# Scaling softmax weights with diagonal matrices on TensorE, and pairing complex products on VectorE, in a one-core decoder layer

## The chip, the cores and the metric

The kernel runs on one core of one Trainium2 chip. The metric is the device time of one execution in microseconds (us); the median of three runs is compared. One further execution was recorded by the hardware profiler, and all rows below are from it. The engines are named as in the profile: PE is TensorE (PEld its weight loads), DVE VectorE, ACT ScalarE, POOL GpSimd, SP SyncE.

## The reference, cut to what matters

The layer has 512 tokens of width 1024 and one depth. An attention with three branches (compressed, selected, window) and a state-space model run side by side on the normalised input; their outputs are mixed, and a channel mixer (PEER) picks 128 experts per token out of 16384. With 512 tokens every selection block is kept, so the selected and the window branch are both causal attention over all earlier tokens. The lines that the change touches compute this:

```
e = where(mask, exp(s - max(s)), 0);  p = e / max(sum(e), 1e-30)      # softmax of a branch
o = gate * (p @ v)                                                  # 8 heads, 2 kv heads
lam_bar = exp(lam * dt)                                             # complex, 32 groups x 64 states
b_bar = ((lam_bar - 1) / lam) * bmat
state[t] = lam_bar * state[t-1] + b_bar @ u[t];  y[t] = Re(cmat @ state[t])
h = h + concat(attention, ssm) @ w_out
h = h + sum over 8 heads x 16 experts of gelu(x . u_e) * gate_e * v_e  # PEER
```

## The kernel before, in words

Tokens are cut into four blocks of 128 (T = 0 to 3). The Python code emits instructions in an order of its own, and a list scheduler, which works with a timing model of the chip, then puts the instructions of each engine into a fixed order. Only the dense stage at the end is kept in program order (`ordered`). Scratch memory comes from slots: `M.L` is a slot of 2048 columns, `M.S` a quarter of one, and who takes a slot waits for whoever used it last.

The stages, in order of time:

- **Parameters and the first block (about 0 to 220 us).** `Half` (two objects, 16 state-space groups each) builds from the parameters the tables PB (b_bar times powers of lam_bar; steps i = 2, 1, 0), CL (the same for c, on POOL) and MT (powers of the unit part of lam_bar, doubled in seven steps k = 0 to 6, each 8 x 2^k columns wide). PB and MT are made on DVE by `cmul`, six VectorE operations for one complex product. Meanwhile PE projects the input. `compress` makes the compressed keys of block 0; it begins with four additions of a position table (`c_peT`) on DVE, in whose output 32 matrix products on PE are waiting. Then come the state-space output, block 0's attention, its mix and its routing.
- **The rest, woven with PEER (about 220 to 735 us).** `rest` projects the other blocks, runs attention(1), the mix of block 1, then the routing of block 1 woven with attention(2) and attention(3), and at last the routing of blocks 2 and 3. Between these, steps of `peer` are emitted by a credit that each piece of work earns. One step gathers a row of `uv` for each of 128 tokens (1 MB, an indirect DMA issued by POOL), takes a dot product on DVE (the operation that writes `junk` and `hid`), five short ACT operations (`gt`, `act`) and a multiply-add on DVE, or from the 109th step on a product on PE (`dg`). Five slots hold gathered rows; a gather is issued two steps ahead, and the multiply-add runs two steps behind.
- **The dense stage (about 850 us to the end).** Blocks 2 and 3 go through all experts by matrix products; 113 steps of block 1 are spread through it.

Inside `attention(T)`, for each of the four pairs (kv head g, branch br), `scores` makes for four heads the scores on PE, their maximum on DVE (`nm`), the exponential with its sum on ACT (`Pt`, `sm`), and three small DVE operations that turn the sums into factors sm. It then multiplies each head's weights (128 rows x N = 128(T+1) columns) by its column of factors: on DVE for T = 0, 1, 2, on ACT for T = 3 (`PSC`). `pv` transposes each 128 x 128 piece of `Pt` on PE against the identity matrix (`c_ident`), copies four of them out of PSUM and multiplies by the values.

Of the kernel before, what the change touches and what calls it, by code (L numbers as in the profile page):

```python
# [18 lines left out]
AF = mybir.ActivationFunctionType  # L19
ALU = mybir.AluOpType  # L20
# [143 lines left out]
def hymba_kernel(ctx: ExitStack, tc: tile.TileContext, a, out, dbg=None):  # L164
# [94 lines left out]
    def cmul(e, outr, outi, xr, xi, yr, yi, t1, t2):  # L259
        e.tensor_tensor(t1, xr, yr, op=ALU.mult)  # L260
        e.tensor_tensor(t2, xi, yi, op=ALU.mult)
        e.tensor_tensor(outr, t1, t2, op=ALU.subtract)
        e.tensor_tensor(t1, xr, yi, op=ALU.mult)
        e.tensor_tensor(t2, xi, yr, op=ALU.mult)
        e.tensor_tensor(outi, t1, t2, op=ALU.add)


    lam = const("lam", [128, 3, 16])
    gmask = const("gmask", [128, 2], eng=G)
# [10 lines left out]
    ident = const("ident", [128, 128])  # L280
# [134 lines left out]
    class Half:  # L415


        def __init__(self, hf, small):
# [11 lines left out]
            cmul(V, pb4[0], pb4[1], br, bi, wr, wi, s1.v(sh4), s2.v(sh4))  # L430
            lbr = lb[:, 0, hs, None].to_broadcast([128, 8, 32])
            lbi = lb[:, 1, hs, None].to_broadcast([128, 8, 32])
            for i in (2, 1, 0):
                cmul(V, PB[0][:, :, i], PB[1][:, :, i], PB[0][:, :, i + 1], PB[1][:, :, i + 1], lbr, lbi,
                     s1.v([128, 8, 32]), s2.v([128, 8, 32]))

            CL = [c.v([128, 8, 5, 32]) for c in self.cl]
            gm = gmask[:, None, :, None].to_broadcast(sh4)
# [12 lines left out]
            MT = [self.mt.v([128, 8, 128], off=4096 * i) for i in range(2)]  # L451
            V.memset(MT[0][:, :, 0:1], 1.0)
            V.memset(MT[1][:, :, 0:1], 0.0)
            for k in range(7):
                n = 1 << k
                sh = [128, 8, n]
                cmul(V, MT[0][:, :, n:2 * n], MT[1][:, :, n:2 * n], MT[0][:, :, 0:n], MT[1][:, :, 0:n],
                     am[:, k, 0, hs, None].to_broadcast(sh), am[:, k, 1, hs, None].to_broadcast(sh), s1.v(sh), s2.v(sh))
# [226 lines left out]
    kcF, vcF = ct("kcF", [128, 2, 31]), ct("vcF", [31, 2, 64])  # L685


    PSC = lambda T, h: T > 2
    PCP = lambda T, kb: T < 3 and kb % 2
    AT, ST, XN, EI, GA = {}, {}, {}, {}, {}  # L690

    def attention(T):
# [13 lines left out]
        sh = [128, 8, n31]  # L706
# [14 lines left out]
        def scores(g, br):  # L721
            pl = M.S() if T == 0 else M.L((0, 1))
            Pt = pl.v([128, 4, N])
            nm = tiny.tile([128, 4], F32, name="nm")
            sm = tiny.tile([128, 4], F32, name="sm")
            for h in range(4):
                par, i = h % 2, h // 2
                ps = bank()
                rows = slice(64 * par, 64 * par + 64)
                PE.matmul(ps[:, 0:N], qT[T][rows, 2 * g + i], KT[rows, 2 * br + g, 0:N], start=True, stop=False)  # L730
                PE.matmul(ps[:, N - 128:N], identb, maskb, start=False, stop=True)
                V.reduce_max(nm[:, h:h + 1], ps[:, 0:N], axis=AX.X, negate=True)
                S.activation(Pt[:, h], ps[:, 0:N], AF.Exp, bias=nm[:, h:h + 1], accum_out=sm[:, h:h + 1])
                bfree(ps)
            V.tensor_scalar(sm, sm, 1e-30, None, op0=ALU.max)
            V.reciprocal(sm, sm)
            V.tensor_tensor(sm, sm, gts[:, T, 4 * g:4 * g + 4, 1 + br], op=ALU.mult)
            for h in range(4):
                if PSC(T, h):
                    S.activation(Pt[:, h], Pt[:, h], AF.Copy, scale=sm[:, h:h + 1])  # L740
                else:
                    V.tensor_scalar(Pt[:, h], Pt[:, h], sm[:, h:h + 1], None, op0=ALU.mult)
            return pl, Pt

        def pv(g, br, pl, Pt):
            for kb in range(T + 1):
                b = bank()
                pt = b3(b, 128)
                for h in range(4):
                    PE.transpose(pt[:, 2 * (h % 2) + h // 2], Pt[:, h, kb * 128:kb * 128 + 128], ident)  # L750
                ps = M.S()
                PT = ps.v([128, 4, 128])
                if PCP(T, kb):
# [6 lines left out]
                              PT[:, 2 * par:2 * par + 2], start=(br == 0 and kb == 0), stop=False, skip_group_check=True)  # L760
                M.free(ps)
                yield
            M.free(pl)

        prev = None
        for g in range(2):
# [884 lines left out]
```

## Time and profile before

| what | value |
|---|---|
| median of 3 runs | 1618.69 us (1617.03 to 1622.68) |
| the profiled execution's own time | 1620.03 us |
| its span, first to last instruction | 1618.2 us |
| PE, DVE, ACT, POOL busy | 1367.1, 1475.7, 837.0, 521.8 us |
| instructions | 24071 |

The busy times are sums over stages with different limits, so they say little by themselves; what counts is which engine is full in a stage and what the chain of waits runs through there. A PE that is called busy need not run at its peak: PEclk is the clock granted to it as a share of full speed, 1.0 for 2.4 GHz and 0.5 for 1.2 GHz.

### The profile page before, as it was taken

To read this page: it belongs to the slowest core of one execution; us is meant where nothing else is said; L and a number is where in the kernel's file an instruction comes from. 1 tells how busy PE (TensorE), PEld (TensorE's weight loads), DVE (VectorE), ACT (ScalarE), POOL (GpSimd) and SP (SyncE) were. 2 spreads that over 40 slices of the span, in tenths; PEclk is the share of its full clock that TensorE was granted. 3 is DMA by queue.
4 is the path that set the end of the run, shared out by engine and by line. 5 is a ranking of instruction groups with operands and counts; after the bars stand their busy time and mean duration, and the time that the engine had idled before them with its cause. 6 is when DMAs were issued, how large, how long until landed. Compare 5 with 4: busy or idle time off the path is not lost.

```text
span 1618.2 us, 24071 instructions
## 1 busy us (share of the span) xinstructions
PE 1367.1 (84%) x8256; PEld 1081.8 (67%) x8256; DVE 1475.7 (91%) x3392; ACT 837.0 (52%) x2046; POOL 521.8 (32%) x383
## 2 busy tenths in 40 slices
PE   5687794588946689696579999999999999999996
PEld 2366572454433455682358888888888999999995
DVE  8986279969899999699999999999999999999998
ACT  2335523545455675225565555555555556555553
POOL 6422013745354233003002333333333433333331
PEclk9897898787877789899859999999999999999998
DMA  6331478888998989309707999999999999999994
GB/s 263 104 105 65 169 278 295 330 321 300 375 352 297 345 356 370 152 6 343 248 4 262 338 345 332 342 337 340 333 346 357 392 375 377 374 375 379 375 376 171
DMA packets 88967, 469.45 MB, mean 290 GB/s; under 512 B 10253, under 2 KB 10893, under 8 KB 50701
## 3 DMA queue, kind: packets, MB, share of 16 engines
q0 software_dynamic: 37152, 268.98, 42.7%
q1 hardware_dynamic: 51692, 198.94, 34.3%
q8 instruction: 64, 1.05, 0.2%
q14 instruction: 59, 0.48, 0.1%
HBM read 464.74 MB, written 3.15 MB: 289 GB/s over the span
## 4 chain that ended last, share of the span: by engine, by line
DVE 46%; PE 29%; issue 12%; DMA 6%; ACT 3%; POOL 3%; SPq 0%; DVEq 0%; POOLq 0%; ACTq 0%
PE bank L134 29%; DVE X L134 27%; DVE lo L134 8%; DVE junk L134 7%; DMA X<-in_uv,eidx 5%; POOL X L134 2%; ACT X L134 2%; DVE act L134 1%; DVE nm L134 1%; DVE more L134 1%; DMA X<-in_x 0%; ACT gt L134 0%; DMA raw<-in_uvt 0%; DVE zT L134 0%; DVE hid L134 0%
## 5 line engine op out<-in xcount | busy, mean ns | idle before, releaser
L134 POOL DMA_INDIRECT X<-in_uv,eidx x256 | 431.6, 1686 | 967.0 <-DVE X L134 854.1
L134 ACT ACTIVATE X<-bank 128x256 f32<-128x256 f32 (+5 forms) x423 | 213.4, 518 | 184.0 <-PE bank L134 134.3
L134 PE MATMUL bank<-hi,act 128*128 128x512 f32 x1024 | 299.7, 394 | 0.0
L134 PE MATMUL bank<-XH,hi 128*128 128x256 f32 x1024 | 288.9, 282 | 4.1 <-ACT hi L134 4.1
L134 PE MATMUL bank<-XH,lo 128*128 128x256 f32 x1024 | 287.8, 281 | 0.0
L134 PE MATMUL bank<-XL,hi 128*128 128x256 f32 x1024 | 287.5, 281 | 0.0
L134 PE MATMUL bank<-X 128*128 128x64 f16 (+10 forms) x1768 | 235.9, 283 | 59.6 <-DVE X L134 39.7
L134 DVE CUSTOM_DVE_ANT_0 junk<-X 128x1024 bf16<-128x1024 f32 x206 | 250.8, 1217 | 14.0 <-DMA X<-in_uv,eidx 11.0
L134 ACT ACTIVATE gt<-hid 128x1 f32<-128x1 f32 x384 | 63.8, 198 | 363.1 <-DVE hid L134 362.9
L134 DVE TENSOR_TENSOR X<-X 128x256 f32<-128x256 f32 (+13 forms) x611 | 230.6, 410 | 22.5 <-ACT X L134 19.7
L134 DVE SCALAR_TENSOR_TENSOR X<-X,act 128x1024 f32<-128x1024 f32 x194 | 247.6, 1276 | 3.6 <-ACT act L134 3.6
L134 DVE TENSOR_TENSOR lo<-raw,hi 128x1024 fp32r<-128x1024 f32 x172 | 209.4, 1217 | 2.8 <-ACT hi L134 2.8
L134 PEld LDWEIGHTS bank<-hi,act 128*128 128x128 f32 x1024 | 183.3, 188 | 32.6
L134 PEld LDWEIGHTS bank<-XH,hi 128*128 128x128 f32 x1024 | 193.9, 189 | 9.1 <-ACT hi L134 4.2
L134 PEld LDWEIGHTS bank<-XL,hi 128*128 128x128 f32 x1024 | 193.3, 189 | 4.9
L134 PE MATMUL bank<-X,X 128*128 128x128 f32 (+7 forms) x888 | 177.1, 373 | 20.9 <-ACT X L134 12.9
L134 PEld LDWEIGHTS bank<-XH,lo 128*128 128x128 f32 x1024 | 194.2, 190 | 0.0
L134 ACT ACTIVATE hi<-raw 128x1024 fp32r<-128x1024 f32 x172 | 179.0, 1053 | 27.4 <-PE bank L134 21.8
L134 PEld LDWEIGHTS bank<-X,X 128*128 128x128 f32 (+4 forms) x888 | 119.8, 194 | 66.2 <-issue 29.7
L134 PE MATMUL bank<-lo,act 128*128 128x512 f32 x512 | 159.5, 393 | 0.4 <-DVE lo L134 0.4
L134 PEld LDWEIGHTS bank<-X 128*128 128x128 f32 (+3 forms) x744 | 117.5, 197 | 54.9 <-issue 28.5
L134 PE MATMUL bank<-c_ident,X 128*128 128x128 f32 (+2 forms) x300 | 55.6, 337 | 85.4 <-DVE X L134 49.4
(202 smaller groups left out, 1775.2 us busy)
## 6 DMA issues: line engine op xcount, KB each, us to landing
raw<-in_uvt SPq DMA_DIRECT2D x172, 512.0 KB, 7.0
X<-in_uvt SPq DMA_DIRECT2D x84, 512.0 KB, 6.7
X<-in_wq SPq DMA_DIRECT2D x24, 1024.0 KB, 8.9
X<-in_wo SPq DMA_DIRECT2D x8, 1024.0 KB, 7.7
X<-in_x SPq DMA_DIRECT2D x8, 512.0 KB, 3.7
X<-in_wB SPq DMA_DIRECT2D x4, 1024.0 KB, 12.8
X<-in_wA SPq DMA_DIRECT2D x4, 1024.0 KB, 5.2
X<-in_w SPq DMA_DIRECT2D x4, 1024.0 KB, 5.5
```

What stands on the lines that cost most here:

```text
L134: ins = self.last = f(*args, **kw)
```

## The change

There are two edits.

1. For T = 1, 2, 3 the weights are no longer multiplied by their factors. Instead ACT makes, for each head, a 128 x 128 diagonal matrix of the factors (the identity scaled by `sm`, in a new slot `dl`), and `pv` multiplies each piece of `Pt` by that diagonal matrix where it was transposed against the identity before. The product transposes and scales at once. T = 0 stays as it was, and `PSC` is gone.
2. `cmul2` computes a complex product with a real part and an imaginary part that stand behind each other, in four DVE operations: two products of double width and two sums. It takes the place of `cmul` in the three PB steps and in MT's steps k = 0 to 5; k = 6, whose products would not fit the scratch slot, keeps `cmul`.

```diff
+    def cmul2(out, x, yr, yi, t1, t2):
+
+        V.tensor_tensor(t1, x, yr, op=ALU.mult)
+        V.tensor_tensor(t2, x, yi, op=ALU.mult)
+        V.tensor_tensor(out[:, 0], t1[:, 0], t2[:, 1], op=ALU.subtract)
+        V.tensor_tensor(out[:, 1], t1[:, 1], t2[:, 0], op=ALU.add)
...
+            sh = [128, 2, 8, 32]
+            PP = self.pb.v([128, 2, 8, 4, 32])
             for i in (2, 1, 0):
-                cmul(V, PB[0][:, :, i], PB[1][:, :, i], PB[0][:, :, i + 1], PB[1][:, :, i + 1], lbr, lbi,
-                     s1.v([128, 8, 32]), s2.v([128, 8, 32]))
+                cmul2(PP[:, :, :, i], PP[:, :, :, i + 1], *(lb[:, n, None, hs, None].to_broadcast(sh) for n in range(2)),
+                      s1.v(sh), s2.v(sh))
...
-            for k in range(7):
+            MM = self.mt.v([128, 2, 8, 128])
+            for k in range(6):
+                n = 1 << k
+                sh = [128, 2, 8, n]
+                cmul2(MM[:, :, :, n:2 * n], MM[:, :, :, 0:n], *(am[:, k, i, None, hs, None].to_broadcast(sh) for i in range(2)),
+                      s1.v(sh), s2.v(sh))
+            for k in (6,):
...
-    PSC = lambda T, h: T > 2
...
+            dl = None if T == 0 else M.S()
             for h in range(4):
-                if PSC(T, h):
-                    S.activation(Pt[:, h], Pt[:, h], AF.Copy, scale=sm[:, h:h + 1])
+                if T == 0:
+                    V.tensor_scalar(Pt[:, h], Pt[:, h], sm[:, h:h + 1], None, op0=ALU.mult)
                 else:
-                    V.tensor_scalar(Pt[:, h], Pt[:, h], sm[:, h:h + 1], None, op0=ALU.mult)
-            return pl, Pt
-
-        def pv(g, br, pl, Pt):
+                    S.activation(dl.v([128, 4, 128])[:, h], ident, AF.Copy, scale=sm[:, h:h + 1])
+            return pl, Pt, dl
+
+        def pv(g, br, pl, Pt, dl):
+
             for kb in range(T + 1):
...
-                    PE.transpose(pt[:, 2 * (h % 2) + h // 2], Pt[:, h, kb * 128:kb * 128 + 128], ident)
+                    o, p = pt[:, 2 * (h % 2) + h // 2], Pt[:, h, kb * 128:kb * 128 + 128]
+                    if T == 0:
+                        PE.transpose(o, p, ident)
+                    else:
+                        PE.matmul(o, p, dl.v([128, 4, 128])[:, h], start=True, stop=True)
```

The scheduler draws up a new order for every engine. Two places matter here.

The first is DVE at the end of `Half`, where the second half's MT steps and the `c_peT` additions of `compress` meet (row widths are columns; 128x8x16 is a sum of step k = 4). Before:

```order
L134 TENSOR_TENSOR X<-X 128x64 x2
L134 TENSOR_TENSOR X<-X 128x8x8
L134 TENSOR_TENSOR X<-X 128x64 x2
L134 TENSOR_TENSOR X<-X 128x8x8
L134 TENSOR_TENSOR X<-X 128x128 x2
L134 TENSOR_TENSOR X_77<-X,c_peT 128x112 x2
L134 TENSOR_TENSOR X<-X 128x8x16
L134 TENSOR_TENSOR X<-X 128x128 x2
L134 TENSOR_TENSOR X_77<-X,c_peT 128x112 x2
```

With the change, the same place:

```order
L134 TENSOR_TENSOR X<-X 128x128 x2
L134 TENSOR_TENSOR X<-X 128x8x8 x2
L134 TENSOR_TENSOR X<-X 128x256 x2
L134 TENSOR_TENSOR X<-X 128x8x16 x2
L134 TENSOR_TENSOR X<-X 128x512 x2
L134 TENSOR_TENSOR X_77<-X,c_peT 128x112
L134 TENSOR_TENSOR X<-X 128x8x32 x2
L134 TENSOR_TENSOR X_77<-X,c_peT 128x112
L134 TENSOR_TENSOR X<-X 128x512 x2
L134 TENSOR_TENSOR X_77<-X,c_peT 128x112 x2
```

The `c_peT` additions stood inside step k = 4 and now stand behind it, among the steps k = 5 and k = 6.

The second place is attention(2), where the first weights are scaled. DVE before (`ISA junk,hid` is the dot product of a PEER step, `X<-X_77,act,X` a multiply-add):

```order
L134 RECIPROCAL sm<-sm 128x4
L134 SCALAR_TENSOR_TENSOR X<-X_77,act,X 128x1024
L134 TENSOR_SCALAR X<-X,sm 128x384 x2
L134 TENSOR_TENSOR sm<-sm,gts 128x4
L134 TENSOR_SCALAR X<-X,sm 128x384 x2
L134 ISA junk,hid<-X_77,X 128x1024
L134 ISA hid 128x1
L134 TENSOR_REDUCE nm<-bank_83 128x1
L134 TENSOR_REDUCE nm<-bank_90 128x1
L134 TENSOR_SCALAR X<-X,sm 128x384 x4
```

With the change, DVE and, under it, ACT (where `c_ident,sm` makes the diagonal matrices):

```order
L134 RECIPROCAL sm<-sm 128x4
L134 TENSOR_TENSOR sm<-sm,gts 128x4
L134 SCALAR_TENSOR_TENSOR X<-X,act 128x1024
L134 TENSOR_TENSOR sm<-sm,gts 128x4
L134 TENSOR_REDUCE nm<-bank_83 128x1
L134 ISA junk,hid<-X_77,X 128x1024
L134 ISA hid 128x1
L134 TENSOR_REDUCE nm<-bank_90 128x1
```

```order
L134 ACTIVATE gt<-hid 128x1 x2
L134 ACTIVATE gt<-hid,ga_1267 128x1
L134 ACTIVATE X_77<-c_ident,sm 128x128 x4
L134 ACTIVATE X_78<-bank_84 128x512
L134 ACTIVATE gt<-gt,hid 128x1
L134 ACTIVATE X_77<-c_ident,sm 128x128 x4
L134 ACTIVATE act<-gt 128x1
L134 ACTIVATE gt<-hid 128x1 x2
```

The wide multiplications have left DVE, and short scalings stand on ACT inside a PEER step's chain of `gt` and `act`.

## Rows read from the trace of the kernel before

**Rows 1.** The page's head: span, and busy time of each engine.

```profile
span 1618.2 us, 24071 instructions
...
PE 1367.1 (84%) x8256; PEld 1081.8 (67%) x8256; DVE 1475.7 (91%) x3392; ACT 837.0 (52%) x2046; POOL 521.8 (32%) x383
```

**Rows 2.** Windows: stretch, length, busy PE, PEld, DVE, ACT, POOL; PEclk, DMA share, GB/s.

```profile
0.00:90.00 90.00, 53.69 (x136) 26.61 (x136) 81.17 (x311) 26.03 (x72) 48.12 (x79) 0.92 0.44 165
...
375.00:400.00 25.00, 22.18 (x92) 13.05 (x93) 25.00 (x58) 14.40 (x58) 15.84 (x6) 0.76 0.90 328
400.00:465.00 65.00, 42.61 (x134) 19.84 (x133) 57.73 (x106) 26.14 (x104) 28.48 (x21) 0.77 0.93 365
465.00:515.00 50.00, 36.14 (x198) 23.53 (x197) 49.08 (x104) 29.85 (x110) 19.44 (x14) 0.84 0.88 329
515.00:620.00 105.00, 81.46 (x392) 50.49 (x391) 100.22 (x240) 68.53 (x230) 36.63 (x30) 0.81 0.88 337
...
850.00:1618.00 768.00, 740.98 (x5094) 669.21 (x5093) 746.55 (x1070) 435.83 (x803) 254.42 (x125) 0.99 0.92 344
```

**Rows 3.** The chain that ended last, 0 to 225 us: start, length, what.

```profile
25.53 27.28 DVE X L134 x76
...
90.09 11.60 PE bank L134 x82
```

**Rows 4.** Timeline of DVE, 20 to 92 us: start, length, operation, count.

```profile
27.99 5.75 DVE L134 TENSOR_TENSOR X<-X 128x256 f32<-128x256 f32 x10
...
67.04 1.29 DVE L134 TENSOR_TENSOR X<-X 128x512 f32<-128x512 f32 x2
...
75.55 0.76 DVE L134 TENSOR_TENSOR X<-X,X 128x256 f32<-128x256 f32 x2
...
85.06 4.72 DVE L134 TENSOR_TENSOR X<-X 128x8 f32<-128x8 f32 x21
```

**Rows 5.** DVE groups by shape, 165 to 670 us: count, busy us, mean ns, idle before.

```profile
L134 DVE TENSOR_SCALAR X<-X,sm 128x384 f32<-128x384 f32 x16 | 5.7, 415 | 0.0
...
L134 DVE TENSOR_SCALAR X<-X,sm 128x256 f32<-128x256 f32 x16 | 4.5, 335 | 0.0
```

**Rows 6.** ACT groups by shape, 165 to 670 us.

```profile
L134 ACT ACTIVATE X<-X,sm 128x512 f32<-128x512 f32 x16 | 10.2, 710 | 2.3 <-DVE sm L134 2.2
...
L134 ACT ACTIVATE dg<-c_ident,act 128x128 f32<-128x128 f32 x3 | 1.2, 397 | 0.1
```

**Rows 7.** Timeline of PE: 140 to 222, 470 to 482, 556 to 572, 584 to 600 us.

```profile
170.50 3.78 PE L134 MATMUL bank<-X,X 128*128 128x128 f32 x16 [4.52 <-ACT X L134]
...
471.40 5.58 PE L134 MATMUL bank<-X,X 128*128 128x128 f32 x48
...
568.19 0.65 PE L134 MATMUL bank<-more,X 128*64 128x256 f32 x4
...
586.74 3.68 PE L134 MATMUL bank<-c_ident,X 128*128 128x128 f32 x16 [4.73 <-ACT X L134]
...
597.51 1.04 PE L134 MATMUL bank<-c_ident,X 128*128 128x128 f32 x8
598.38 0.39 PE L134 MATMUL bank<-X,X 128*128 128x128 f32 x2
```

**Rows 8.** Windows of two stretches, 470 to 478 and 556 to 568 us.

```profile
470.00:478.00 8.00, 8.00 (x61) 6.60 (x59) 7.76 (x17) 5.14 (x20) 3.58 (x3) 1.00 0.96 354
556.00:568.00 12.00, 7.02 (x32) 6.30 (x32) 12.00 (x29) 10.23 (x29) 3.94 (x3) 0.50 0.75 260
```

**Rows 9.** The chain that ended last, 375 to 625 us.

```profile
391.57 13.71 DMA X<-in_uv,eidx
...
464.35 7.51 PE bank L134 x32
...
525.21 10.87 DMA X<-in_uv,eidx
...
592.18 32.41 PE bank L134 x164
```

More of the change, by code (lines that the diff above doesn't have):

```diff
@@ L762, in pv @@
                 yield
-            M.free(pl)
+            M.free(pl, *([dl] if dl else []))
         prev = None
```

## The prediction

> **What bounds the kernel now.** I read the page's head first: DVE is the fullest engine with 1475.7 us of 1618.2, PE follows with 1367.1 [rows 1]. Such shares mix stages, so the table of windows comes next. From 850 us on, the dense stage runs with PE at 741 of 768 us [rows 2]. Neither edit touches an instruction there, so it keeps its length, and what the change is worth is by how much it moves that stage's start. Before it, DVE is the full engine. In the first 90 us it is busy for 81 [rows 2], and the chain of waits runs on DVE from 25.5 us, with one piece of 27.3 us, until at 90.1 PE takes over with `compress` [rows 3]. In the attention stretches DVE is busy for 25.0 of 25 us (T = 1, 375 to 400), 49.1 of 50 (most of T = 2, 465 to 515) and 100.2 of 105 (T = 3, 515 to 620), while PE idles there for 2.8, 13.9 and 23.5 us, and ACT for more [rows 2]. The reader should see that PE has room in T = 2 and T = 3, and hardly any in T = 1. The chain in these stretches still holds more than DVE: gathers in flight (13.7 us from 391.6, 10.9 us from 525.2) and PE (7.5 us from 464.4, 32.4 us from 592.2) [rows 9].
>
> **Complex products: from 36 operations fewer.** Each step with `cmul2` saves two operations; per half there are three PB steps and six MT steps, so 2 x 9 x 2 = 36 go. The columns that DVE works through stay the same, only each operation's fixed part goes. Two 256-column operations in a row take 0.76 us, two of 512 take 1.29 us [rows 4]. Merging four of 256 into two of 512 therefore turns 1.52 us into 1.29: 0.115 us for each operation removed, and 36 x 0.115 = 4.1 us is the lower price. The narrow steps cost mostly their fixed part: 21 operations take 4.72 us, 0.225 each [rows 4]. With 0.225 for the 20 narrow ones and 0.115 for the other 16, it is 4.5 + 1.8 = 6.3 us. While POOL builds CL beside it, a 256-column operation takes 0.575 us [rows 4]; since no such row exists for 512 columns, I don't use that.
>
> Part of this is given back by the new order. The `c_peT` additions, for which `compress` waits, now stand behind the rest of step k = 4 and the products of k = 5: two narrow sums (0.45 us), two products of 512 columns (1.29) and some wider products, some 2 us by [rows 4]. The start of PE's 11.6 us piece [rows 3] moves up by 4.1 - 2 = 2.1 to 6.3 - 2 = 4.3 us. I take 3 us. The ends for the range are 0 (what follows to 220 us, where PE, ACT and POOL pass work on in turn, absorbs it) and 6.3 (the table MT decides, not `compress`).
>
> **Scaling leaves DVE in T = 1 and 2.** 32 operations go: 4.5 us with 256 columns and 5.7 us with 384, together 10.2 us [rows 5]. In T = 2 DVE is full and PE is not, so I count all 5.7. In T = 1 the gathers already move 328 GB/s, and 4.5 us less would ask for 328 x 25 / 20.5 = 400; the next stretch, which is full of gathers, moves 365 [rows 2]. So I count half, 2.3. Together 8 us; ends 0 and 10.2.
>
> **ACT** gets 48 scalings of 128 columns, at most 0.40 us each by the nearest row (`dg`, the identity scaled by a column), 19 us, and loses 16 of 512 columns, 10.2 us [rows 6]: 9 us more in 245 us of which it idles for 106 [rows 2]. In T = 3 the four scalings ahead of the transposes shrink from about 2.6 us to 1.6 or less; that only feeds a PE which waits for DVE elsewhere, so I take nothing. There is a new wait: ACT, in order, waits for the DVE operations that make sm, and the PEER step's `gt` and `act` stand behind the scalings. Its multiply-add on DVE is two steps behind its dot product; that slack hides 1.6 us, and if it were gone the 8 scaling groups of T = 1 and 2 would cost at most 8 x 1.6 = 13 us. I take nothing.
>
> **PE** does a product where it did a transpose, 144 times (16 in each of the nine pieces: 2 + 3 + 4). A transpose is recorded as one MATMUL, a product of this type as two: the two value products of a piece are four MATMULs [rows 7]. At full clock eight transposes begin at 597.51 and the next instruction at 598.38, so each takes 0.11 us; 48 MATMULs of the same size take 5.58, 0.116 each. So a product costs 0.232 instead of 0.11, 0.12 us more. At half clock 16 transposes take 3.68 us (0.23) and 16 MATMULs 3.78 (0.236) [rows 7]: 0.24 more. The 144 cost PE 17 to 35 us, of which 32 stand in T = 1, 48 in T = 2, 64 in T = 3. The room in T = 2 and 3 (13.9 and 23.5 us) takes their 6 to 12 and 8 to 15 us. On the chain I find 16 transposes in PE's piece from 592.2 [rows 7, 9]: 16 x 0.12 = 2 us. I take 2, ends 0 and 35.
>
> The Trainium skill (TensorE: Matmul & The Clock Gate, Terms) says that the transpose mode makes an fp32 transpose four times as fast; by that 144 products would cost three times 0.11 us more each, 47 us, where the rows give 17. The trace differs, and the sum goes by the rows.
>
> **Sum.** 1620.0 (the profiled execution's own time) - 3 - 8 + 2 = 1611. The median of the runs lies 1.3 us below the profiled time, so I predict 1610 us.
>
> **Rivals.** *The gathers set the pace.* From 375 to 620 us the DMA engines are 88 to 93% busy [rows 2], and five slots pass through gather, dot and multiply-add. If a faster DVE only waits longer for rows, the 8 us are gone: 1618.7 - 3 + 2 = 1618. For it speak the two DMA pieces of the chain [rows 9]; against it that DVE idles for only 0.9 us of 50 in T = 2, and that the stretch before moves 365 GB/s against 329 there [rows 2].
>
> *PE becomes the bound of attention (slower).* The place is `pv`: ACT's copies, the value products and the next scores stand behind 0.24 us more per head and piece. It decides once more than 11 us of the 35 fall on the chain; with half of them, 17.5, the time is 1618.7 - 11 + 17.5 = 1625. For it: transposes run mostly at half clock, and T = 1 has 2.8 us of room for 4 to 8 us. Against it: PE's idle time in T = 2 and 3.
>
> *The clock rises.* From 556 to 568 us PE is busy for 7.0 of 12 us with 32 transposes alone, and the granted clock stays at 0.50 throughout, while eight full microseconds of products have 1.00 [rows 8]. If products lift the clock where transposes did not, 64 MATMULs at full clock take 7.4 us, as long as the 32 transposes, so the PE term is 0, and the products after such a stretch run faster: the piece at 592.2 begins at half clock for some 3 us and would save 1.5. Time: 1618.7 - 11 - 1.5 = 1606. The same is what the Trainium skill (TensorE: Matmul & The Clock Gate, Part 4: PE-mode transpose) states, that transposes do not count as work for the clock; the rows agree as far as they go.
>
> *The change does less than it says in the first stage:* `compress` is held back as much as DVE is relieved, and that term is 0: 1618.7 - 8 + 2 = 1613.
>
> **How the numbers follow.** About 5 us (0.3%) is what a measurement can tell from no change. Forecast: 0.50, by itself 1604 to 1615. Gathers: 0.22, 1618. PE: 0.13, 1625 or more. Clock: 0.10, 1606. First stage: 0.05, 1613. Faster than 1613.8: 0.43 of the forecast's 0.50, the clock's 0.10, half of the last 0.05, so 0.56. Slower than 1623.5: PE's 0.13 and a tail of the gathers, 0.15. Same: 0.29. The range leaves out 2 in 10: at its low end 1600, the best ends of the terms (1618.7 - 6.3 - 10.2 - 1.5 = 1601), at its high end 1624, which holds the gathers and leaves out most of PE's case.
>
> **What would show it.** The start of PE's `compress` piece 2 to 4 us earlier. No DVE group on `X<-X,sm` of 256 or 384 columns, and all that follows attention(3), the start of the dense stage too, some 9 us earlier. ACT with 48 groups of about 0.3 to 0.4 us on `c_ident,sm`. PE with 288 MATMULs of 128 columns at 0.116 us or twice that, and the granted clock in those bursts. Dense stage of equal length. The prediction is wrong if DVE's idle time from 375 to 620 us grows by what it was relieved of (then a gather, a PE or an ACT row must stand before the idle time), or if the new order of the last routing costs or gives more than these terms.

## The result and the profile after

The changed kernel took 1602.01 us (median; 1595.86 to 1603.72), the kernel before beside it 1620.68 us (1617.03 to 1624.07): a ratio of 0.9871, 95% interval 0.9845 to 0.9897. Measured once more later, the same two gave 1606.32 and 1622.05, 0.9896 (0.9871 to 0.9922). So the change takes off 17 to 21 us. The forecast was 9 us off the profiled time, and 1610 us.

One correction first: the text ahead of the prediction says that 113 steps of block 1 are spread through the dense stage. The trace shows 128 dot products there, all of block 1; the 15 that stand just before it are the last steps of block 0.

The head of the page after, and the ACT groups that answer to [rows 1, 6] (165 to 655 us):

```profile
span 1602.0 us, 24306 instructions
...
PE 1374.4 (86%) x8400; PEld 1094.4 (68%) x8400; DVE 1460.7 (91%) x3324; ACT 838.6 (52%) x2078; POOL 524.4 (33%) x383
```

```profile
L134 ACT ACTIVATE X<-c_ident,sm 128x128 f32<-128x128 f32 x44 | 13.9, 388 | 1.2 <-DVE X L134 0.6 <-DVE sm L134 0.5
L134 ACT ACTIVATE more<-c_ident,sm 128x128 f32<-128x128 f32 x4 | 1.3, 399 | 0.0
```

DVE lost 15.0 us, PE gained 7.3 and 144 MATMULs, and the groups of [rows 5] are gone. The windows that answer to [rows 2] (the last one 16 us earlier, as the dense stage is):

```profile
375.00:400.00 25.00, 25.00 (x131) 15.49 (x130) 21.44 (x38) 15.82 (x62) 12.43 (x9) 1.00 1.01 403
400.00:465.00 65.00, 44.88 (x171) 24.72 (x170) 59.03 (x111) 30.07 (x120) 27.37 (x19) 0.76 0.89 344
465.00:515.00 50.00, 47.53 (x300) 32.43 (x299) 48.72 (x118) 35.45 (x129) 16.78 (x14) 0.97 0.89 340
515.00:620.00 105.00, 83.74 (x376) 48.66 (x375) 99.26 (x223) 58.80 (x216) 43.54 (x32) 0.85 0.89 346
...
834.00:1602.00 768.00, 741.26 (x5093) 669.84 (x5091) 746.57 (x1070) 435.56 (x803) 252.41 (x125) 0.99 0.92 344
```

From 375 us the gathers now move 403 GB/s where they moved 328, DVE is no longer full there, and PE has a clock of 1.00 in place of 0.76. But the work has moved by up to 20 us inside such fixed windows, so that they hold other instructions than those of [rows 2]. Between its own events, from its first scores to the first scores of T = 2, block T = 1 has changed much less (before, then after):

```profile
349.48:432.68 83.20, 77.41 (x300) 42.70 (x301) 69.47 (x145) 41.06 (x154) 38.76 (x23) 0.82 0.82 311
```

```profile
344.37:424.91 80.54, 78.32 (x332) 46.48 (x333) 64.54 (x127) 44.31 (x166) 34.12 (x23) 0.86 0.82 316
```

It is 2.7 us shorter, the gathers move 316 GB/s in place of 311, and the clock is 0.86 in place of 0.82. For the budget I therefore cut both traces at the same events: the first gather, the last sum that writes XL (when the inputs of the last routing are ready) and the last `dg` product. Before, and then after:

```profile
0.00:220.10 220.10, 161.17 (x794) 110.80 (x795) 155.71 (x525) 83.63 (x211) 71.20 (x102) 0.88 0.40 145
220.10:666.00 445.90, 322.27 (x1441) 198.29 (x1440) 411.08 (x1090) 233.88 (x834) 177.99 (x138) 0.81 0.87 335
666.00:784.80 118.80, 99.44 (x389) 68.59 (x388) 102.44 (x556) 44.43 (x159) 17.30 (x17) 0.99 0.40 147
784.80:1618.20 833.40, 784.20 (x5637) 704.10 (x5635) 806.45 (x1225) 475.08 (x843) 255.37 (x126) 0.96 0.87 325
```

```profile
0.00:216.10 216.10, 158.87 (x795) 109.90 (x796) 150.01 (x489) 83.83 (x211) 74.64 (x103) 0.90 0.41 147
216.10:652.40 436.30, 330.59 (x1587) 210.96 (x1586) 398.51 (x1042) 233.01 (x853) 177.72 (x138) 0.84 0.88 340
652.40:767.40 115.00, 99.49 (x384) 67.96 (x383) 103.12 (x563) 46.25 (x170) 18.09 (x17) 0.96 0.41 156
767.40:1602.00 834.60, 785.40 (x5640) 705.61 (x5638) 809.01 (x1233) 475.49 (x845) 253.96 (x127) 0.96 0.87 325
```

This is the budget of the change: -4.0 us to the first gather, -9.6 to the last XL sum, -3.8 to the last `dg` product, +1.2 behind it: -16.2 in all. I call the two middle windows together **the stretch**: 564.7 us before, 551.3 after. DVE's busy time in it fell from 513.5 to 501.6 us, by 11.9 (10.2 of it the scalings of [rows 5]); its idle time went from 51.2 to 49.7. The rest of the 11.9 is work that moved: behind the last `dg` product DVE now has 1233 operations in place of 1225, and 2.6 us more to do. So DVE's relief was handed on in full, and PE's 144 products added nothing to DVE's waiting. In the 3.8 us behind the XL sums a hole became smaller: DVE's MAX8 operations wait for the query products of the last routing, 15.2 us before (first row) and 11.5 after (second row):

```profile
L134 DVE MAX8 X<-bank 128x8 f32<-128x128 f32 x16 | 4.6, 289 | 15.2 <-PE bank L134 15.2
```

```profile
L134 DVE MAX8 X<-bank 128x8 f32<-128x128 f32 x32 | 8.9, 287 | 11.5 <-PE bank L134 11.5
```

In the first stage `compress` starts on PE at 88.14 us, 2.0 earlier than in [rows 3]:

```profile
88.14 3.45 PE L134 MATMUL bank<-X,X 128*14 128x128 f32 x30 [2.43 <-DVE X L134]
```

The chain of waits of this trace can be followed back only to 752.6 us, so there is nothing to set beside [rows 9]. In its place stand the waits in the PE groups, 340 to 640 us, first of before, then of after:

```profile
L134 PE MATMUL bank<-X,X 128*128 128x128 f32 x222 | 34.2, 313 | 4.2 <-DMA X<-in_wq 4.2
...
L134 PE MATMUL bank<-c_ident,X 128*128 128x128 f32 x160 | 31.8, 369 | 54.3 <-DVE X L134 37.1 <-ACT X L134 12.0 <-POOL X L134 5.2
```

```profile
L134 PE MATMUL bank<-X,X 128*128 128x128 f32 x528 | 75.0, 304 | 5.2 <-DMA X<-in_wq 5.2
...
L134 PE MATMUL bank<-X 64*128 64x512 f32 x32 | 20.1, 711 | 15.8 <-DVE X L134 14.3 <-ACT X L134 1.5
```

Not all of the 37.1 us that the group `c_ident,X` waits for DVE belongs to the weights. One wait stands ahead of eight transposes that the change leaves alone, and it is still there (before, then after):

```profile
464.35 1.97 PE L134 MATMUL bank<-c_ident,X 128*128 128x128 f32 x8 [22.25 <-DVE X L134]
```

```profile
453.64 1.97 PE L134 MATMUL bank<-c_ident,X 128*128 128x128 f32 x8 [20.12 <-DVE X L134]
```

So the weights' transposes had PE waiting for 14.9 us on DVE and 12.0 on ACT. Their products stand in the `X,X` group, before which PE waits for nothing but a load; one wait of 14.3 us for DVE has come up ahead of the scores of T = 3. And the clock pays for part of the products. Two pairs of MATMULs of T = 1's scores, before and after, [rows 7]' columns:

```profile
379.60 1.22 PE L134 MATMUL bank<-X 64*128 64x256 f32 x2
```

```profile
374.70 0.70 PE L134 MATMUL bank<-X 64*128 64x256 f32 x2
```

The first ran at a granted clock of 0.50, the second at 1.00.

### The profile page after: what moved, and what is told of

Its sections match the earlier page's. It is cut to its first block, busy times and chain, and to the rows that moved or that the text cites. A ratio compares the mean times of both kernels' runs of the same rounds, so it can differ in the third digit from the quotient of the medians.

```text
span 1602.0 us, 24306 instructions
## 1 busy us (share of the span) xinstructions
PE 1374.4 (86%) x8400; PEld 1094.4 (68%) x8400; DVE 1460.7 (91%) x3324; ACT 838.6 (52%) x2078; POOL 524.4 (33%) x383
## 4 chain that ended last, share of the span: by engine, by line
DVE 25%; PE 22%; issue 4%; ACT 1%; DMA 1%; SPq 0%
PE bank L134 22%; DVE X L134 11%; DVE lo L134 8%; DVE junk L134 3%; DVE act L134 2%; DMA raw<-in_uvt 1%; ACT X L134 0%; DVE f_r L134 0%; DVE hid L134 0%; ACT hi L134 0%; ACT junk L134 0%; ACT raw L134 0%; DVE more L134 0%; ACT act L134 0%; SPq L1255 0%
## 5 line engine op out<-in xcount | busy, mean ns | idle before, releaser
L134 ACT ACTIVATE X<-bank 128x256 f32<-128x256 f32 (+5 forms) x431 | 218.0, 520 | 181.7 <-PE bank L134 130.6
L134 PE MATMUL bank<-X 128*128 128x64 f16 (+10 forms) x1800 | 243.2, 285 | 71.0 <-DVE X L134 50.0
L134 PE MATMUL bank<-X,X 128*128 128x128 f32 (+5 forms) x1172 | 209.9, 352 | 21.3 <-ACT X L134 11.8
L134 PEld LDWEIGHTS bank<-X,X 128*128 128x128 f32 (+3 forms) x1172 | 150.3, 195 | 67.4 <-issue 28.4
L134 PEld LDWEIGHTS bank<-X 128*128 128x128 f32 (+3 forms) x776 | 123.7, 197 | 67.9 <-issue 29.6
L134 PEld LDWEIGHTS bank<-lo,act 128*128 128x128 f32 x512 | 95.9, 188 | 22.7 <-DVE lo L134 0.8
```

The costliest lines, as they stand in the source:

```text
L134: ins = self.last = f(*args, **kw)
```

## Experiments

All ratios are to the kernel before on the same chip. "Stretch", busy and idle time of DVE in it, and the clock (granted from the first gather to the last XL sum) are of the one profiled execution, whose own time stands beside them.

| kernel | median us | ratio (95%) | profiled us | first gather | stretch | DVE busy | DVE idle | clock |
|---|---|---|---|---|---|---|---|---|
| before | 1620.68 | | 1620.0 | 220.1 | 564.7 | 513.5 | 51.2 | 0.81 |
| changed | 1602.01 | 0.9871 (0.9845-0.9897) | 1603.7 | 216.1 | 551.3 | 501.6 | 49.7 | 0.84 |
| changed_again | 1606.32 | 0.9896 (0.9871-0.9922) | 1606.7 | 217.2 | 553.6 | 502.3 | 51.3 | 0.83 |
| cmul_only | 1618.45 | 0.9986 (0.9968-1.0003) | 1618.5 | 215.1 | 569.0 | 515.0 | 54.0 | 0.80 |
| diag_only | 1609.31 | 0.9927 (0.9908-0.9946) | 1609.2 | 220.0 | 553.1 | 501.8 | 51.3 | 0.84 |
| slot_only | 1618.50 | 0.9987 (0.9972-1.0001) | 1618.4 | 218.2 | 564.5 | 510.5 | 54.0 | 0.79 |
| ident_products | 1632.85 | 1.0060 (1.0041-1.0080) | 1636.0 | 219.0 | 581.1 | 515.5 | 65.6 | 0.82 |
| scale_on_dve | 1626.07 | 1.0039 (1.0014-1.0064) | 1632.2 | 217.3 | 577.8 | 513.3 | 64.5 | 0.80 |
| dve_work_back | 1624.90 | 1.0009 (0.9990-1.0028) | 1628.7 | 219.1 | 574.1 | 511.3 | 62.8 | 0.81 |
| dve_hop | 1606.92 | 0.9906 (0.9887-0.9926) | 1603.4 | 215.6 | 551.1 | 504.7 | 46.4 | 0.84 |
| dve_beside2 | 1609.10 | 0.9924 (0.9898-0.9951) | 1604.1 | 214.2 | 555.0 | 510.2 | 44.8 | 0.83 |
| dve_beside | 1641.11 | 1.0115 (1.0094-1.0135) | 1636.6 | 215.8 | 583.6 | 508.7 | 74.9 | 0.86 |
| products_twice | 1615.36 | 0.9951 (0.9932-0.9970) | 1617.2 | 220.7 | 560.5 | 501.8 | 58.7 | 0.87 |
| act_scale | 1616.02 | 0.9954 (0.9935-0.9973) | 1614.2 | 218.7 | 560.9 | 506.4 | 54.5 | 0.79 |
| act_scale_again | 1617.08 | 0.9981 (0.9963-1.0000) | 1627.2 | 222.1 | 570.2 | 505.7 | 64.5 | 0.78 |
| act_scale_cmul | 1612.52 | 0.9942 (0.9921-0.9962) | 1610.5 | 215.9 | 559.8 | 505.7 | 54.1 | 0.81 |
| wide_products | 1619.90 | 0.9989 (0.9968-1.0009) | 1624.0 | 222.6 | 565.4 | 506.6 | 58.8 | 0.83 |
| t1_wide | 1611.14 | 0.9912 (0.9881-0.9943) | 1611.7 | 220.8 | 555.9 | 503.8 | 52.1 | 0.82 |
| t3_as_before | 1604.81 | 0.9884 (0.9863-0.9906) | 1604.4 | 216.3 | 553.2 | 504.8 | 48.4 | 0.82 |

**How far a profile repeats.** Two kernels were run twice.

> The changed kernel once more, on the chip of the two runs beside it: 1600 to 1605 us, and in the profile the same lengths as in its first profile within 2 us (first gather at 216 us, 551 us from there to the last dg product, 834 us from there to the end). If these lengths differ by more, differences of that size between the other runs say nothing.

> The kernel of act_scale once more, on the same chip: 1613 to 1619 us, 561 us from the first gather to the last dg product and a clock of 0.79 as in its first profile, within 2 us and 0.01.

The first repeats within 1.1 us at the first gather and 2.3 in the stretch. The second does not: its profiled execution took 10 us more than its median, and the stretch is 9.3 us longer, all of it DVE's idle time; DVE's busy time repeats to 0.7 us. So below, verdicts rest on medians. An idle time belongs to its own execution, and says less where the profiled time in the table lies some us from the median, as in ident_products, dve_work_back, dve_hop, dve_beside, dve_beside2, scale_on_dve and wide_products (3 to 6 us).

**Each part alone.** The complex products:

```diff
+                cmul2(PP[:, :, :, i], PP[:, :, :, i + 1], *(lb[:, n, None, hs, None].to_broadcast(sh) for n in range(2)),
...
+                cmul2(MM[:, :, :, n:2 * n], MM[:, :, :, 0:n], *(am[:, k, i, None, hs, None].to_broadcast(sh) for i in range(2)),
```

> Edit 2 alone: cmul2 in the parameters, attention as before. The order of all engines behind the first stage is that of before. My account (the whole first-stage gain is this edit, and it travels to the end): the first gather of PEER starts 4 us earlier than before, at about 216 us, and the time falls by 4 us, to 0.9975 of before. Rival (PE, ACT and the gathers behind it absorb it): first gather 4 us earlier, end within 1 us of before, 1.000. Rival (the two edits help each other): less than 2 us.

The diagonal matrices:

```diff
+                    S.activation(dl.v([128, 4, 128])[:, h], ident, AF.Copy, scale=sm[:, h:h + 1])
+                        PE.matmul(o, p, dl.v([128, 4, 128])[:, h], start=True, stop=True)
```

> Edit 1 alone: diagonal matrices in attention, cmul as before. My account (10 us of DVE work gone in T = 1 and 2 in full, 3 us in the last routing): nothing changes up to 220 us; from the first gather to the first query product of the last routing 10 us less (442 before), the last routing up to the last dg product 3 us less (123 before), the time 13 us lower, 0.992 of before. Rival (the gathers pace the attention stretch): 3 us or less, 0.998.

The stretch of each (to the last XL sum, then to the last `dg` product):

```profile
215.10:663.50 448.40, 327.18 (x1439) 201.61 (x1438) 411.33 (x1090) 234.05 (x834) 180.60 (x138) 0.80 0.88 333
663.50:784.10 120.60, 102.31 (x391) 69.74 (x390) 103.69 (x558) 44.35 (x159) 17.39 (x17) 0.96 0.41 148
```

```profile
220.00:656.70 436.70, 329.50 (x1580) 209.14 (x1580) 398.61 (x1042) 233.33 (x853) 177.22 (x138) 0.84 0.89 339
656.70:773.10 116.40, 101.39 (x390) 69.21 (x389) 103.17 (x563) 46.26 (x170) 17.57 (x17) 0.96 0.41 153
```

Alone, the complex products give 0.14% (2 us, with nothing that rules out zero). They bring the first gather 5.0 us forward, and 4.3 of it is lost again in the stretch, 2.8 as idle time of DVE. The diagonal matrices alone take 11 us off (0.73%), with DVE's budget of the stretch that of the changed kernel. Beside them the complex products are worth another 0.31 to 0.56% (5 to 9 us, by the two runs of the changed kernel), of which the profile shows 4 at the first gather.

**Only the slot and the order.** The diagonal matrices need a new quarter slot, and that alone redraws the scheduler's order:

```diff
-            return pl, Pt
+            return pl, Pt, (None if T == 0 else M.S())
```

> Before, with one more quarter slot taken for each pair in attention(1 to 3) and freed behind pv, and nothing written to it: no operation is added or removed, only slots and so the scheduler's order change. In the last routing it has the order of the changed kernel, heads of blocks 2 and 3 in step. My account: the last routing, from its first query product to the last dg product, is 3 us shorter (123 before), the rest within 2 us, the time 1 to 5 us lower, 0.997 to 0.999. Rival (the new order is worth most of the extra gain): 8 us lower or more. Rival (orders don't matter): 1.000.

It gives 0.13%, 2 us, with nothing that rules out zero. The order of the last routing is nearly that of the changed kernel here, so that order is not where the gain came from. It does shift work between the windows of the budget: with that slot in T = 3 the last routing takes 113.9 to 117.2 us in ten profiles, without it 118.8 to 121.4 in eight (dve_beside apart), and here the 2.1 us by which it became shorter are spent ahead of it, 447.8 in place of 445.9 us. So the 3.8 us of the last routing are no gain that stands by itself.

**What the products cost PE.** Products in the kernel before, by the plain identity (DVE still scales T = 1 and 2):

```diff
-                    PE.transpose(pt[:, 2 * (h % 2) + h // 2], Pt[:, h, kb * 128:kb * 128 + 128], ident)
+                        PE.matmul(o, p, ident, start=True, stop=True)      # T > 0
```

> Before, with each transpose of a weight piece for T = 1 to 3 replaced by a product with the identity matrix; DVE and ACT scale as before. It has PE's side of edit 1 and none of DVE's relief. My account (PE has room, and products raise the granted clock where transposes left it at 0.5): the 144 products cost nothing on the chain, the time is within 3 us of before, and the granted clock from 500 to 610 us is above the 0.80 of before. Rival (my predicted PE term): 2 us slower. Rival (PE bounds attention): 9 to 17 us slower, 1.006 to 1.010. Rival (the clock is what brought the extra gain): 4 us faster or more.

10 us slower (0.60%); in a profiled execution 3 us above the median, DVE's idle time is up by 14 us and its work by 2. My own account, that the products cost nothing on the chain, fell here; the rival was right in size. The products of the changed kernel twice:

```diff
                         PE.matmul(o, p, dl.v([128, 4, 128])[:, h], start=True, stop=True)
+                        PE.matmul(o, p, dl.v([128, 4, 128])[:, h], start=True, stop=True)
```

> The changed kernel with every product by a diagonal matrix issued twice into the same bank (the second repeats the first): PE gets 144 products more, 33 us at full clock and up to 68 at half, and no other engine gets anything. Theory A (DVE is the bound and PE's products lie beside it, as the prediction had it): at most 4 us slower, 1606 us. Rival B (PE's products lie mostly on the chain of attention, as in the kernel before with identity products, which lost 12 us for half as much): 12 to 25 us slower, 1614 to 1627 us.

0.55 to 0.80% slower (9 to 13 us). PE's busy time up to the last XL sum is 27 us above that of the changed kernel's, DVE's idle time 9 above; 4.6 us of the profile's loss stand before the first gather, in instructions that the edit does not touch. A second set of products is thus neither free nor fully on the chain.

**Giving DVE its work back.** In the changed kernel, first as a multiplication by 1.0 in place, and then as a tiny one that makes the products wait for DVE but is little work:

```diff
+                    if T < 3:
+                        V.tensor_scalar(Pt[:, h], Pt[:, h], 1.0, None, op0=ALU.mult)                      # dve_work_back
+                        V.tensor_scalar(Pt[:, h, ::128], Pt[:, h, ::128], 1.0, None, op0=ALU.mult)        # dve_hop
```

> The changed kernel, but DVE again multiplies the weights of T = 1 and 2 (here by 1.0, 32 operations, 10.2 us), and the diagonal matrices stay. Theory A (the relief of DVE pays, about one for one or more): 10 to 16 us slower, 1612 to 1618 us. Rival B (what pays is something else, the order or the clock): within 4 us, 1606 us or less.

> The changed kernel, with 32 tiny DVE multiplications (by 1.0) in T = 1 and 2 that touch two or three columns of each head's weights, one in each piece, so that every product waits for DVE again: some 2 us of work in place of 10.2. Theory A (DVE's work is what counts): 1602 to 1606 us. Rival B (the passage through DVE's queue counts): 1610 to 1620 us, with PE waiting for DVE in T = 2 and the granted clock of 465 to 515 us at 0.8 as in the kernel before, not 0.97.

The work in place costs 18 to 22 us, twice its busy time. The tiny operation costs 2 to 6, with 3.1 us more of DVE's busy time. So passing through DVE's queue is not expensive by itself; at 1606.92 us the run ended between the two forecasts, far nearer to A. Then the work beside the path, with its result read by nothing:

```diff
+                        V.tensor_scalar(junk.bitcast(F32)[:, 0:N], Pt[:, h], 1.0, None, op0=ALU.mult)     # dve_beside
+                        V.tensor_scalar(pl.v([128, N], off=16 * N), Pt[:, h], 1.0, None, op0=ALU.mult)    # dve_beside2
```

> The changed kernel, and DVE again does 32 multiplications of the weights' columns in T = 1 and 2 (by 1.0), but writes them to a spare place that nothing reads; the products on PE take the weights as ACT left them. So DVE has the 10.2 us of work back, and the weights don't pass through DVE's queue. Theory A (DVE's work is what was relieved; giving it back into the queue cost 22 us because everything there waits): 1615 us or more. Rival B (the passage through DVE's queue between ACT's exponential and PE cost more than the work): 1605 to 1612 us.

> As dve_beside, but the 32 multiplications write into columns of the weights' own slot that nothing else uses, so that no PEER dot product is put behind them (in dve_beside they shared its output, and the gathers started 70 us late). DVE has 10.2 us of work back that nothing waits for. Theory A (DVE's work counts one for one, wherever it stands): the stretch from the first gather to the last dg product 9 to 12 us longer than in the changed kernel (551.4 us), with DVE's idle time there as it was (48 us), 1611 to 1616 us. Rival B (work that nothing waits for finds room): within 4 us, 1606 us or less.

The first told nothing about this: its results went to the place where the dot products write, which put the PEER steps behind them (the 21st dot product began at 380 us, 71 later), and it took 1641.11 us against 1623.38. The second cost 0.28% beside changed_again on the same chip (4.5 us, the intervals overlap): less than theory A wanted, and half of the 8.6 us by which DVE's busy time grew. At last, the scaling as before and products by the identity in T = 1 and 2, T = 3 as in the changed kernel:

```diff
-                if T == 0:
+                if T < 3:
                     V.tensor_scalar(Pt[:, h], Pt[:, h], sm[:, h:h + 1], None, op0=ALU.mult)
+                        PE.matmul(o, p, dl.v([128, 4, 128])[:, h] if T == 3 else ident, start=True, stop=True)
```

> The changed kernel, with the scaling of T = 1 and 2 on DVE as before (32 operations, by sm), products with the plain identity there, T = 3 with diagonal matrices. Theory A (one for one): 1611 to 1616 us. Rival B (scaling in DVE's queue makes PE, with its longer products, wait too, and DVE's idle time grows as with identity products in the kernel before, +13 us, and with the work back, +13): 1620 to 1627 us.

20 us slower than changed_again on the same chip. The waits of its PE, 340 to 640 us, are near those of before: of the 34.3 us below, 22.7 are again the wait of the eight other transposes, and 11.7 stand ahead of the weights' products.

```profile
L134 PE MATMUL bank<-X,X 128*128 128x128 f32 x224 | 38.5, 343 | 8.6 <-DMA X<-in_wq 7.8 <-ACT X L134 0.9
...
L134 PE MATMUL bank<-c_ident,X 128*128 128x128 f32 x176 | 30.5, 340 | 36.8 <-DVE X L134 34.3 <-POOL X L134 2.5
```

Work alone costs 4.5 us, passing through the queue alone 2 to 6, both together about 20. What costs, by these runs, is that full-width scalings on DVE stand between the exponential and PE. Each of these edits also redraws the order, and how the loss comes about inside the queue no run took apart.

**Scaling on ACT in full width, transposes kept.** The kernel before with one table changed, then with the complex products as well:

```diff
-    PSC = lambda T, h: T > 2
+    PSC = lambda T, h: T > 0
```

> The kernel before, with one table changed: ACT instead of DVE multiplies the weights in T = 1 and 2 as well, in their full width (32 operations of 256 and 384 columns leave DVE); the transposes stay. Theory A (what pays in the diagonal edit is that 10.2 us leave DVE): at least as fast as the kernel with the diagonal edit alone, 1603 to 1611 us, since PE's dearer products are not there. Rival B (ACT's wide scalings stand in front of the transposes and of PEER's gt and act; the diagonal matrices pay because they are short): 1616 us or more, with idle time of PE behind ACT's X<-X,sm.

> The kernel with the scaling on ACT in full width for T = 1 to 3 and transposes on PE, and the complex products in four operations as well. Alone the complex products gave 2 us of the 5 that they gain before the first gather; beside the diagonal matrices about 7. Theory A (once DVE no longer scales the weights, the start of the attention is passed on to its end): 5 to 7 us less than with the scaling on ACT alone (1616 us there), 1609 to 1611 us. Rival B (the difference is the scheduler's luck, not a rule): 1613 to 1616 us.

DVE has lost its scalings, as in the changed kernel, but only 0.19 to 0.46% is gained (3 to 7 us), and theory A missed. ACT's scalings are long here, 340 to 640 us:

```profile
L134 ACT ACTIVATE X<-X,sm 128x512 f32<-128x512 f32 x16 | 10.2, 710 | 0.9 <-DVE sm L134 0.9
L134 ACT ACTIVATE X<-X,sm 128x384 f32<-128x384 f32 x16 | 8.4, 602 | 0.6 <-DVE sm L134 0.6
L134 ACT ACTIVATE X<-X,sm 128x256 f32<-128x256 f32 x16 | 6.8, 498 | 0.4 <-DVE sm L134 0.4
```

25.4 us, where the diagonal matrices take 15.2. One scaling takes 498 to 710 ns, a diagonal matrix 388. The Trainium skill (ScalarE: Activation LUTs, What ACT_TABLE_LOAD costs) gives some 280 ns and 0.833 ns for each column where one operand has one value per row; these rows agree, and show that the length goes by the columns. The complex products add 0.12 to 0.39% to it; whether a rule is behind that or the order stays open. Now the same with products by the identity in place of the transposes, in nearly the same order:

```diff
-    PSC = lambda T, h: T > 2
+    PSC = lambda T, h: T > 0
+                        PE.matmul(o, p, ident, start=True, stop=True)      # T > 0
```

> As act_scale (ACT multiplies the weights of T = 1 to 3 in full width, nothing passes through DVE), but PE multiplies the pieces by the plain identity where act_scale transposes them. ACT's and DVE's work is that of act_scale; 144 transposes become products, and hardly anything in the order changes. Theory A (with no DVE in between, products lift the granted clock where transposes did not, and cost nothing): the clock from the first gather to the last XL sum 0.82 or more in place of 0.79, PE busy within 4 us of act_scale's 329, the time 0 to 8 us less, 1608 to 1616 us. Rival B (a product costs PE 0.12 to 0.24 us more wherever it stands): PE busy 17 us more or above, the time 8 to 16 us more, 1624 us or above.

The two to the last XL sum, act_scale and then wide_products:

```profile
218.70:658.50 439.80, 329.01 (x1433) 198.92 (x1432) 400.29 (x1053) 241.88 (x850) 170.55 (x138) 0.79 0.89 338
```

```profile
222.60:666.60 444.00, 332.40 (x1577) 212.10 (x1576) 400.66 (x1054) 242.50 (x850) 177.30 (x138) 0.83 0.88 334
```

144 MATMULs more, 3.4 us more of PE's busy time (2.8 less than in the twin, act_scale_again), a clock of 0.83 in place of 0.79 (0.78 in the twin): the clock pays for nearly all of the products. The Trainium skill (TensorE: Matmul & The Clock Gate, Part 4: PE-mode transpose) says that transposes do not count as work for the clock; this pair agrees. The time is 0.08% above that of the twin on the same chip (1 us, not to be told from none), though not below 1616 us as theory A had it; by the ratio of the first act_scale, from another chip, it would be 0.35% (6 us).

Between wide_products (0.9989) and diag_only (0.9927) 10 us are left, with intervals that don't meet. Products and relief are alike, and the diagonal matrix is shorter: ACT is busy for 233 us in place of 242 up to the last XL sum. That its shortness brings the 10 us is not shown. The quarter slot differs too, which by itself gave 2, and the order does: compared by operation, names and shapes, over a quarter of DVE's operations stand in another place. No run has short and long scalings in the same order, and the next two, which take one block each, show little of it.

**Which block needs it.** The changed kernel, with T = 1, and with T = 3, on ACT in full width and transposed:

```diff
+                if T == 1:                                                                   # t1_wide; T == 3 in t3_as_before
+                    S.activation(Pt[:, h], Pt[:, h], AF.Copy, scale=sm[:, h:h + 1])
+                    if T in (0, 1):                                                          # T in (0, 3) in t3_as_before
                         PE.transpose(o, p, ident)
```

> The changed kernel, but in T = 1 ACT multiplies the weights in their full width (256 columns, about as long as a diagonal matrix) and PE transposes them as before; diagonal matrices stay in T = 2 and 3. In T = 1 the changed kernel's PE is full (25.0 of 25 us from 375), so if its 32 products lie on the chain, 4 to 8 us come back: 1595 to 1599 us, faster than the changed kernel. Rival (gathers set the pace there, their DMA share is 1.01 in those 25 us): 1600 to 1604 us.

> The changed kernel, but T = 3 as before: ACT multiplies the 512 columns of each head and PE transposes; diagonal matrices stay in T = 1 and 2. Nearly the whole order of the engines stays. Between the last scores of T = 2 and those of T = 3 the changed kernel had gained 8.5 us more on the kernel before. Theory A (those 8.5 us are the relief of DVE in T = 1 and 2 handed on): within 3 us of the changed kernel, 1600 to 1605 us. Rival B (T = 3 itself pays: four scalings of 1.6 instead of 2.6 us ahead of each piece's products, and a higher clock): 1607 to 1612 us, with the granted clock lower and PE waiting for ACT between 500 and 560 us.

T = 3 alone brings at most 2 us (0.9884 lies between the changed kernel's 0.9871 and 0.9896), although a scaling became shorter there than anywhere else, 388 for 710 ns. t1_wide lost 3 to 7 us, but not in T = 1: between its own events that block takes 80.8 us, in the changed kernel 80.5. In its profile 4.7 us of the loss stand before the first gather, in instructions that the edit does not touch, and the rest behind T = 1. The 4 to 8 us that I hoped to win back in T = 1 weren't there either. In the fixed window from 375 us the clock is 0.81 with transposes, where the changed kernel had 1.00; over the whole block it is 0.81 and 0.86:

```profile
375.00:400.00 25.00, 23.77 (x102) 13.14 (x102) 21.43 (x41) 17.61 (x66) 11.16 (x8) 0.81 0.96 346
```

No version tried is clearly faster than the changed kernel.

## Why the prediction was wrong in size

**Complex products, -3 us: right.** DVE was busy for 5.7 us less up to the first gather, between the 4.1 and 6.3 of the two prices, and `compress` came 2.0 us earlier, at the edge of the 2.1 to 4.3. At the first gather it is 4.0 us. In the medians they are worth 2 us alone and 5 to 9 beside the diagonal matrices.

**Scaling leaves DVE, -8 us: the term that was mis-sized.** With PE's +2 it made -6 of edit 1; diag_only measured -11, about the whole 10.2 us of the scalings and no price for the products. The step that failed is the count stage by stage, in which relief that does not shorten its own stage was gone. T = 1 alone did become only 2.7 us shorter, near the 2.3 that I had allowed. But its PEER steps are not tied to it, and what was left came later. T = 3, from its first scores to the last product of its compressed branch, became 13.3 us shorter, though DVE lost no scaling there, with 29 dot products in place of 33 (before, then after):

```profile
504.54:624.16 119.62, 88.90 (x424) 55.40 (x424) 114.73 (x270) 73.63 (x252) 43.74 (x35) 0.80 0.88 334
```

```profile
497.81:604.15 106.34, 84.84 (x431) 51.72 (x430) 101.79 (x230) 65.21 (x240) 43.63 (x32) 0.86 0.88 336
```

Over the whole stretch all of it was handed on: DVE's idle time did not grow (51.2 us before, 49.7 and 51.3 with the change). And I counted the scaling as work of DVE alone. dve_work_back shows that the same 10.2 us cost about 20 when they stand between exponential and products; ident_products shows that products in the kernel before, behind DVE's scalings, cost 10. So edit 1 is not a sum of a relief and a price; the two have to be measured together.

**ACT, 0: not refuted.** The "nothing" was said of T = 3, where four short scalings take the place of long ones, and there the change brought at most 2 us (t3_as_before). Relief of DVE by full-width scaling on ACT is worth 3 to 7 us, the diagonal matrices 11; whether their shortness or the order makes the rest stays open, and T = 2 alone wasn't tried.

**PE, +2 us: small as forecast, for another reason.** The 144 MATMULs came, and PE's busy time rose by 8.3 us from the first gather to the last XL sum, below the 17 to 35 of the working. The clock paid for much of it (0.81 to 0.84), and not room alone. That the price came out near nothing is partly luck, since the working had the clock stay. The rival *clock rises* had this mechanism and, at 1606 us, the forecast nearest to the two measured times. *PE becomes the bound* did not come; ident_products and scale_on_dve, which keep DVE's scaling, are as slow as that rival (1632.85 and 1626.07 us), but there DVE's idle time grew by 14 and 13 us. *Gathers set the pace* fell with DVE's idle time, which did not grow.

**Last routing, no term: -3.8 us** (-2.5 in changed_again). The prediction named its new order as what could make it wrong. DVE's wait for PE there shrank from 15.2 to 11.5 us. But the same order came with the slot alone (116.7 us), which gained 2 us in all, so this is in part work that changed sides of the cut.

**Dense stage:** its window of 768 us has the same work in it, [rows 2], and the part behind the last `dg` product became 1.2 us longer.

Open: whether the complex products really pass on more of their gain beside the diagonal matrices than alone (5 to 9 against 2 us, near the scatter of such ratios), and whether the 10 us between wide and short scalings come from their length, and if so by which wait, or from the order.

## What to carry to other kernels

Work of the fullest engine can cost more than its length where it stands between two other engines: here 10.2 us of it cost about 20 on the path and some 4.5 beside it. When moving such work, compare its length in the new place; the short form on ACT gained 11 us, the wide form 3 to 7, though the order differs too. Terms of such a path can't be priced one by one, nor stage by stage where a scheduler moves other work between the stages; put the pair together (scaling and product) before adding it up. And cut two traces at the same events, and add busy and idle time of the fullest engine between them: that budget showed in four windows what fixed windows hid.

## What the runs showed that was not expected

- Products in place of transposes raised the granted clock and so cost PE 3.4 us in place of 17 or more (0.79 to 0.83, wide_products), but not where DVE scaled the weights in full width: there it was 0.82 and 0.80 (ident_products, scale_on_dve; 0.81 in the kernel before), and PE's busy time from the first gather to the last XL sum 21 and 24 us more than in the kernel before.
- DVE's busy time in the stretch repeats to 0.7 us from run to run; its idle time differed by 10.0 us between two profiles of one kernel (act_scale and its twin), whose runs spread from 1611 to 1628 us.
- Instructions that no edit touches, before the first gather, shifted that gather by up to 6.6 us between kernels with the same first stage (214.2 in dve_beside2, 220.8 in t1_wide). It was not the order: by operation, names and shapes PE, DVE, ACT and POOL run the same sequence there. The granted clock differed, most of all from 140 to 150 us (dve_beside2, then t1_wide), and in two executions of one kernel too, 0.83 in act_scale and 0.50 in its twin, whose first gather came 3.4 us later. What set it apart stays open.

```profile
140.00:150.00 10.00, 7.90 (x58) 6.25 (x58) 8.59 (x25) 3.75 (x13) 2.64 (x4) 1.00 0.01 2
```

```profile
140.00:150.00 10.00, 10.00 (x48) 8.92 (x47) 2.36 (x8) 4.02 (x12) 1.59 (x2) 0.56 0.02 7
```
